# A two-layer hybrid encoder on one core: norms and gate rows spread by DMA, the feed-forward's plan started earlier and kept in order

## The chip, the core and the metric

The kernel runs on one core of one Trainium2 chip. The core has a matrix engine (TensorE, "PE" in the profile, with its weight loads as "PEld"), VectorE ("DVE"), ScalarE ("ACT"), GpSimd ("POOL") and SyncE ("SP"), each with an instruction queue of its own that it works through in order. DMAs are issued from the queues of SyncE, ScalarE and GpSimd. The metric is the device time of one execution in microseconds; lower is better.

## What is computed

Everything is float32. The stream has 512 positions of width 1024; there are two layers. Cut to its frame:

```python
for layer in range(2):
    xn = rms_norm(x, mix_norm[layer])
    if layer == 0:      # 8 heads of forgetting attention and 4 of differential attention
        mixed = fox_diff_mixer(xn, ...)
    else:               # 4 mLSTM heads, chunkwise
        mixed = mlstm_mixer(xn, ...)
    x = x + mixed
    x = x + memory_cross_attention(rms_norm(x, xattn_norm[layer]), rms_norm(mem, mem_norm[layer]), ...)
    x = x + conv_ffn(rms_norm(x, ffn_norm[layer]), ...)      # causal 3-tap conv, gelu(g) * u
return rms_norm(x, final_norm)

def rms_norm(x, gain):
    return x * rsqrt(mean(x * x, axis=-1) + 1e-6) * gain
```

The differential heads (each of width 128) and the mLSTM heads (each of width 256) have a norm of the same kind over their own width. The forgetting heads need a running sum of log-forget gates along the sequence, one row of 512 numbers per head; the mLSTM needs for each head a running maximum and a stabilizer, again one row of 512 per head.

## The kernel before

Activations lie transposed: features on the 128 partitions, the 512 positions along the free axis, so x is eight tiles `x[k]` of 128x512. A float32 product is made from three fast ones: every operand is split into a high part and a low remainder (ScalarE casts the high part, VectorE subtracts it: `split`, `sub`, L278 to L283), and `mm3` (L285 to L291) multiplies high by high, low by high and high by low. So each weight tile of 128x1024 costs a load on SyncE's queue (`raw`), a cast on ScalarE (`wh`) and a subtraction on VectorE (`wl`); each of these three has three buffers. Products are gathered in four PSUM banks `acc` and in two pairs of banks with the tags `s` and `w`.

**Order.** The program is unrolled in full. In all stages but the feed-forward, `Plan` (L80) orders work by hand: each item has a duration on TensorE and a chain of durations on ScalarE ("A"), VectorE ("D") and GpSimd ("G"), and takes and frees slots of buffers; `Plan.run` walks along TensorE's time, takes the first ready item by priority and calls its function, which issues the instructions. The feed-forward uses `Sched` (L159): tasks per engine with durations, latencies and slots, in which the engine that can start earliest is served, and ties go by priority. Both fix the order in which instructions are issued. The compiler's own scheduler then places them in the queues by that order and by its own estimate of when an operand is ready, so that a queue's order may differ from the plan's.

**Norm by columns** (`p_norm` L369, `rsqrt_cols`, `rsqrt`, `bcast_cols` L435). The squares of all feature tiles are summed into one tile `sq` on ScalarE and VectorE. Four narrow products per 512 positions sum over the partitions and leave the sums as columns (128x4). `rsqrt` computes the inverse root on VectorE with a first guess by bits and three Newton steps: twelve instructions on 128x4. `bcast_cols` splits the result, multiplies it into two diagonal 128x512 tiles on VectorE, and two wide products with a matrix of ones spread it over all partitions; a copy to SBUF by ScalarE makes `rb` where the result is kept. `self.r`, the columns, serves where positions lie on partitions (values); `self.rb` serves as a factor when products are evacuated (in `query` L1055, in `evac` L1320).

**Rows of gates.** `split_rows` (L594) splits rows into high and low parts in one tile; `bcast_row` (L607) makes a selecting matrix on VectorE and spreads one row with one wide product, and ScalarE copies it out of PSUM: once for each forgetting head (into `ta`), twice for each mLSTM head (`mxb`, and `emt` with an exponential). GpSimd cuts these tiles causally (`affine_select`, L900 and L1576) before they are used in the scores.

**Memory.** `p_memory` (L944) norms the same 256 memory positions in both layers, with each layer's gain; its `memrb` multiplies the keys.

**Feed-forward** (`ffn_steps`). 22 pairs of column blocks (g and u). Pairs 0 to 4 are plain: two blocks of 24 wide products each. From pair 5 on (`seven`) a pair is computed with seven products of a 2x2 scheme, which need sums of weight tiles: a tile `sa` is loaded on SyncE's queue and a second load from GpSimd's queue is added onto it in flight (L1340), and VectorE forms `sb` from it (L1362). The activations for this scheme are formed once (`forms`: tiles `th`, `tl`, by way of the buffers `hs` and `sa`), after pairs 0 and 1. `hs` has two buffers, shared by `forms` and by the pairs' evacuated rows; `sa` has three. After a pair, `tail` convolves (ScalarE, four VectorE taps), applies the gelu and splits. In `seven` ScalarE copies the first product out as `v` (L1394), and the next products wait for it. `fill` puts blocks of the down projection between. The norm of the feed-forward is issued after the first block of pair 0.

## Time and profile before

| | us |
|---|---|
| time, median of three runs (lowest, highest) | 1456.62 (1454.38, 1457.17) |
| profiled execution, its own time | 1456.26 |
| its span, first to last instruction | 1454.5 |
| TensorE busy | 1423.8 (98%) |
| VectorE busy | 1177.4 (81%) |
| ScalarE busy | 826.3 (57%) |
| GpSimd busy | 58.7 (4%) |

The rows shown further down are of that one profiled execution. A row of the timeline has the start and the duration in us, the engine, the line, the operation, the tiles written and read, the shapes, a count, and in brackets the idle time before it with what ended it. A row of the groups has, after the bar, busy time in us and the mean of one instruction in ns. An engine with a q behind its name (SPq) is its queue issuing a DMA. A row of DMA issues ends with KB each and the median us from issue to landing. A row of waits has the waiting instruction, what it waited for, the total in us, how often, and the longest.

### The profile page before, as it was taken

The numbers are of one execution on the slowest core, as the hardware profiler recorded it, in microseconds if no ns is written. First come the engines' busy times: TensorE is split into PE (matmuls) and PEld (weight loads), VectorE is DVE, ScalarE is ACT, GpSimd is POOL, SyncE is SP. The second block draws the span as 40 slices with busy tenths as digits, with TensorE's granted clock in tenths as the row PEclk, the third lists the DMA queues.
The fourth block names the chain that finished last, engine by engine and source line by source line (L and its number), as shares of the span: only waits on it lengthen the run. The fifth ranks groups of instructions, "written<-read, shape, count | busy, mean of one in ns | idle before, by whom it ended". The sixth has DMA issues, their size and how long they took to land.

```text
span 1454.5 us, 22322 instructions
## 1 busy us (share of the span) xinstructions
PE 1423.8 (98%) x8366; PEld 1269.8 (87%) x8366; DVE 1177.4 (81%) x2206; ACT 826.3 (57%) x1416; POOL 58.7 (4%) x101
## 2 busy tenths in 40 slices
PE   9999999999998999999999999999999989999998
PEld 7888868899887999999888788889988889999997
DVE  7778886766687999999778868676667889999985
ACT  7767574444464566666456734445445556666654
POOL 0000120000000000000000100000000000000000
PEclk9999999999999999999999999999999999999999
DMA  5222314323236566652232232323323656666412
GB/s 200 88 73 73 102 32 158 117 86 131 87 123 180 150 167 159 169 156 77 84 102 87 73 102 80 109 93 125 116 87 123 174 153 153 174 154 167 124 59 80
DMA packets 61213, 172.55 MB, mean 119 GB/s; under 512 B 6704, under 2 KB 6704, under 8 KB 61104
## 3 DMA queue, kind: packets, MB, share of 16 engines
q1 hardware_dynamic: 55344, 152.69, 31.9%
q0 software_dynamic: 4752, 17.30, 7.0%
q8 instruction: 66, 1.08, 0.3%
q10 hardware_dynamic: 1008, 1.12, 0.2%
q14 instruction: 43, 0.35, 0.1%
HBM read 168.99 MB, written 2.10 MB: 118 GB/s over the span
## 4 chain that ended last, share of the span: by engine, by line
PE 78%; DVE 13%; ACT 4%; issue 3%; DMA 2%; POOL 0%; SPq 0%; DVEq 0%; ACTq 0%; POOLq 0%
PE acc L289 15%; PE acc L291 14%; PE acc L290 14%; PE w L289 5%; PE w L290 5%; PE w L291 5%; DVE wl L279 3%; PE s L289 2%; PE s L290 2%; PE s L291 2%; PE acc L351 2%; PE acc L352 2%; PE acc L353 2%; DVE c L1285 2%; DMA sa<-in_up_dram 1%
## 5 line engine op out<-in xcount | busy, mean ns | idle before, releaser
L289 PE MATMUL acc<-xh,wh 128*128 128x512 f32 (+1 forms) x824 | 289.2, 351 | 0.0
L291 PE MATMUL acc<-xh,wl 128*128 128x512 f32 (+1 forms) x824 | 285.0, 346 | 0.0
L290 PE MATMUL acc<-xl,wh 128*128 128x512 f32 (+1 forms) x824 | 284.8, 346 | 0.0
L279 DVE TENSOR_TENSOR wl<-raw,wh 128x1024 fp32r<-128x1024 f32 (+2 forms) x200 | 239.3, 1196 | 38.2 <-ACT wh L282 35.7
L282 ACT CAST wh<-raw 128x1024 fp32r<-128x1024 f32 (+2 forms) x137 | 140.3, 1026 | 155.2 <-PE acc L290 95.8
L291 PEld LDWEIGHTS acc<-xh,wl 128*128 128x128 f32 x824 | 156.5, 190 | 14.8
L289 PEld LDWEIGHTS acc<-xh,wh 128*128 128x128 f32 x824 | 156.6, 190 | 14.3
L290 PEld LDWEIGHTS acc<-xl,wh 128*128 128x128 f32 x824 | 156.7, 190 | 14.2
L1285 DVE SCALAR_TENSOR_TENSOR c<-hs,vec,c 128x512 f32<-128x512 f32 x176 | 129.2, 746 | 2.7 <-ACT c L1278 2.6
L289 PE MATMUL w<-ah,wh 128*128 128x512 f32 x304 | 115.7, 381 | 0.0
L290 PE MATMUL w<-al,wh 128*128 128x512 f32 x304 | 115.5, 380 | 0.0
L291 PE MATMUL w<-ah,wl 128*128 128x512 f32 x304 | 115.3, 379 | 0.0
L1278 ACT ACTIVATE c<-hs,vec 128x512 f32<-128x512 f32 x88 | 67.5, 809 | 19.1 <-DVE hs L1422 9.3
L291 PEld LDWEIGHTS w<-ah,wl 128*128 128x128 f32 x304 | 57.6, 189 | 8.2
L289 PEld LDWEIGHTS w<-ah,wh 128*128 128x128 f32 x304 | 58.0, 191 | 6.7
L290 PEld LDWEIGHTS w<-al,wh 128*128 128x128 f32 x304 | 57.9, 190 | 6.6
L289 PE MATMUL acc<-mem,wh 128*128 128x256 f32 (+1 forms) x192 | 60.3, 314 | 0.0
L291 PE MATMUL acc<-mem,wl 128*128 128x256 f32 (+1 forms) x192 | 59.7, 311 | 0.0
L1299 ACT CAST ah<-c 128x512 fp32r<-128x512 f32 x44 | 27.2, 619 | 57.0 <-DVE c L1295 56.9
L290 PE MATMUL acc<-mem,wh 128*128 128x256 f32 (+1 forms) x192 | 59.6, 310 | 0.0
L512 DVE TENSOR_TENSOR x<-w,x 128x512 f32<-128x512 f32 x72 | 49.4, 686 | 7.9 <-PE w L291 7.7
L512 DVE TENSOR_TENSOR x<-acc,x 128x512 f32<-128x512 f32 x32 | 22.0, 690 | 40.4 <-PE acc L291 40.4
(373 smaller groups left out, 3810.3 us busy)
## 6 DMA issues: line engine op xcount, KB each, us to landing
raw<-in_up_dram SPq DMA_DIRECT2D x55, 512.0 KB, 3.2
sa<-in_up_dram SPq DMA_DIRECT2D x33, 512.0 KB, 4.2
sa<-in_up_dram POOLq DMA_DIRECT2D x33, 512.0 KB, 5.5
dr<-in_down_dram SPq DMA_DIRECT2D x64, 256.0 KB, 3.6
ra<-in_up_dram SPq DMA_DIRECT2D x33, 256.0 KB, 3.3
raw<-in_xk_dram SPq DMA_DIRECT2D x16, 512.0 KB, 3.2
raw<-in_wo_dram SPq DMA_DIRECT2D x16, 512.0 KB, 3.2
raw<-in_xq_dram SPq DMA_DIRECT2D x16, 512.0 KB, 3.3
```

What stands on the lines that cost most here:

```text
L279: self.nc.vector.tensor_tensor(out=lo, in0=v, in1=hi.bitcast(F32), op=ALU.subtract)
L282: self.nc.scalar.copy(hi, v)
L289: mm(out, wh, xh, start=first, stop=False, skip_group_check=parts)
L290: mm(out, wh, xl, start=False, stop=False, skip_group_check=parts)
L291: mm(out, wl, xh, start=False, stop=last, skip_group_check=parts)
L351: mm(ps, xh[k][:, ts], wh, start=(k == 0), stop=False)
L352: mm(ps, xh[k][:, ts], wl, start=False, stop=False)
L353: mm(ps, xl[k][:, ts], wh, start=False, stop=(k == 7))
L512: self.nc.vector.tensor_tensor(out=x, in0=restored(ps[:]), in1=x, op=ALU.add)
L1278: nc.scalar.activation(st["c_"][:, j, :], hs()[:, j, 2:514], AF.Identity, scale=self.col("cw", (layer * 3 + 2) * 44 + blk), bias=self.col( ...
L1285: nc.vector.scalar_tensor_tensor(out=c, in0=hs()[:, j, n : n + 512], scalar=w, in1=c, op0=ALU.mult, op1=ALU.add)
L1299: nc.scalar.copy(acts[p][0][:], u())
```

## The change

Eleven norms (four differential heads, three of four mLSTM heads, both cross-attentions, both feed-forwards) are computed by rows, `p_row_norm`: `sq` is split, two wide products with ones give the sums on every partition, ScalarE takes one row out with scale and epsilon, a DMA from ScalarE's queue turns it to 128x4, GpSimd raises it to the power -0.5, and two DMAs from GpSimd's queue write the result to DRAM and read it back spread over 128 partitions. The first VectorE instruction that reads it is pinned behind the one issued before it (`follow`). The norms that stay by columns (first, mixer of layer 1, last mLSTM head, memory of layer 0, final) get the power on GpSimd in place of the Newton steps. The gate rows are written to DRAM once and each is read back spread, by DMA from GpSimd's queue; the exponential of `emt` is taken on the rows. The memory's norm is kept in DRAM for layer 1. The differential heads have two `ta` buffers in place of three, the forgetting rows three `fb` of their own; `mxb` and `emt` have two each. In the feed-forward `Sched` starts each engine's clock ahead of TensorE's (`AHEAD`), models the end of the stage before, puts the norm first, and ScalarE's and VectorE's instructions are chained in the order of the plan (`planned`). Cut to its core:

```diff
...
+ROW_DMA, SPREAD_DMA = 2.7, 6.0
...
+ORDERED = ("vector", "scalar",)
...
             t += pick.dur
             u = t + (0.1 if pick.chain else 0.0)
             for e, d in pick.chain:
+                if e == "-":
+                    u += d
+                    continue
                 u = max(u, eng[e]) + d
...
+AHEAD = {"SP": 14.0, "POOL": 10.0, "ACT": 5.0, "DVE": 5.0}
...
-        self.slots = {r: [0.0] * n for r, n in res.items()}
+        self.slots = {r: [-AHEAD["SP"]] * n for r, n in res.items()}
...
-        now = {e: 0.0 for e in todo}
+        now = {e: -AHEAD.get(e, 0.0) for e in todo}
...
-                    at = 0.0 if e == "-" else now[e]
+                    at = max(t.after, -99.0 if e == "-" else now[e])
...
+class InOrder:
+    def __init__(self, tc, engine):
+        self.tc, self.engine = tc, engine
+        self.on, self.next, self.last = False, False, None
+        self.info = mybir.DependencyInfo(mybir.DependencyClass.NoSync, mybir.DependencyReason.SCHED_ONLY)
+    def __getattr__(self, name):
+        issue = getattr(self.engine, name)
+        def call(*a, **k):
+            i = issue(*a, **k)
+            if self.last is not None and (self.on or self.next):
+                self.tc.add_manual_dep(i.ins, self.last, self.info, reason="planned order")
+            self.last, self.next = i.ins.name, False
+            return i
+        return call
...
+    def follow(self):
+        self.next = True
...
+    def planned(self, on):
+        for c in self.chains:
+            c.on, c.last = on, None
...
+        a = pl.add(parts, 0, deps, prio, chain=(("A", 0.52), ("D", 0.6)))
+        a = pl.add(sums, 0.43, [a], prio, take=("s",), free=("s",), chain=(("A", 0.5),))
+        a = pl.add(turned, 0, [a], prio, chain=(("-", ROW_DMA),))
+        a = pl.add(lambda: st.update(d=self.row_root(st["z"])), 0, [a], prio, chain=(("G", 1.05), ("-", ROW_DMA)))
+        a = pl.add(spread, 0, [a], prio, chain=(("-", SPREAD_DMA),))
...
+        def last():
+            nc.vector.follow()
+            fin(st["rb"])
+        return pl.add(last, 0, [a, *fdeps], prio, chain=chain)
...
+    def row_parts(self, sq):
+        hi, lo = (self.til(self.sp, "sqt", dtype=F32R) for _ in range(2))
+        self.split(hi[:], lo[:], sq[:])
+        return hi, lo
+    def row_sums(self, parts, scale, eps):
+        ps = self.bank("b")
+        for i, part in enumerate(parts):
+            self.nc.tensor.matmul(banked(ps[:]), self.onesr[:], alternate(part[:]), start=i == 0, stop=i == 1)
+        row = self.til(self.sp, "sqt")
+        self.nc.scalar.activation(folded(row[0:1, :]), restored(ps[0:1, :]), AF.Copy, scale=float(scale), bias=float(eps))
+        return row
+    def row_turned(self, row):
+        z = self.til(self.sp, "z", (P, 4))
+        self.nc.scalar.dma_start(z[:], row[0:1, :].rearrange("o (p j) -> o p j", j=4))
+        return z
+    def row_root(self, z):
+        y = self.til(self.sp, "y", (P, 4))
+        self.nc.gpsimd.tensor_tensor(out=y[:], in0=z[:], in1=self.power[:], op=ALU.pow)
+        d = self.til(self.dp, "roots", (1, SEQ))
+        self.nc.gpsimd.dma_start(d[:].rearrange("o (p j) -> (o p) j", j=4), y[:])
+        return d
+    def row_spread(self, d, to):
+        rb = self.til(*to)
+        self.nc.gpsimd.dma_start(rb[:], d[0:1, :].to_broadcast([P, SEQ]))
+        return rb
...
-        nc.vector.tensor_scalar(out=y.bitcast(I32), in0=z.bitcast(I32), scalar1=-0.5, scalar2=1597463007.0, op0=ALU.mult, op1=ALU.add)
-        nc.vector.tensor_scalar(out=zh, in0=z, scalar1=-0.5, scalar2=None, op0=ALU.mult)
-        for _ in range(3):
-            nc.vector.tensor_tensor(out=a, in0=y, in1=y, op=ALU.mult)
-            nc.vector.tensor_tensor(out=a, in0=a, in1=zh, op=ALU.mult)
-            nc.vector.scalar_tensor_tensor(out=y, in0=a, scalar=1.5, in1=y, op0=ALU.add, op1=ALU.mult)
+        nc.gpsimd.tensor_tensor(out=y, in0=z, in1=self.power[:, :nt], op=ALU.pow)
...
+    def spread_cols(self, diags, n, pool, tag, bufs=2):
+        ps = self.bank("b")
+        for i, dg in enumerate(diags):
+            self.nc.tensor.matmul(banked(ps[:, :n]), self.onesr[:], alternate(dg), start=i == 0, stop=i == 1)
...
+        self.power = cp.tile([P, 4], F32, name="power")
+        nc.vector.memset(self.power[:], -0.5)
...
-    def bcast_row(self, rows, c):
-
-        ps = self.bank("b")
-        s = self.til(self.sp, "sel", (P, P), F32R)
-        self.nc.vector.tensor_copy(s[:], self.selc[:, c : c + 1].to_broadcast([P, P]))
-        self.nc.tensor.matmul(banked(ps[:]), s[:], alternate(rows[:]), start=True, stop=True)
-        return restored(ps[:])
-
+    def spread_row(self, rows, c, tile):
+        self.nc.gpsimd.dma_start(tile[:], rows[c : c + 1, :].to_broadcast([P, SEQ]))
...
             def decays():
-                f = self.log_sigmoid_sum(rows["z"], 8, mp, "ta", "tb", "tmp", NTA)
-                rows["f"] = self.split_rows(mp, f)
+                rows["f"] = self.log_sigmoid_sum(rows["z"], 8, mp, "ta", "tb", "tmp", NTA)
+                rows["d"] = self.til(self.dp, "decays", (8, SEQ), bufs=1)
+                nc.gpsimd.dma_start(rows["d"][:], rows["f"])
...
 
                     def spread(h=h, fb=fb):
-                        fps = self.bcast_row(rows["f"], h)
-                        fb["b"] = self.til(mp, "ta", bufs=NTA)
-                        nc.scalar.copy(folded(fb["b"][:]), fps)
-
-                    b = pl.add(spread, MM, [g, *qk], p + SOFT_PRIO, take=("s", "ta"), free=("s",), chain=(("A", 0.5),))
+                        fb["b"] = self.til(mp, "fb", bufs=3)
+                        self.spread_row(rows["d"], h, fb["b"])
+                    b = pl.add(spread, 0, [g], p, take=("fb",), chain=(("-", SPREAD_DMA),))
                     got = pl.add(lambda pt=pt: pt.update(t=self.til(mp, "pt", (P, 1536), bufs=3)), 0, qk, p + SOFT_PRIO, take=("pt",))
...
-                self.squares(k, raw, MEM, state)
+                if layer == 0:
+                    self.squares(k, raw, MEM, state)
...
+            self.memd = self.til(self.dp, "memroots", (1, MEM), bufs=1)
+            nc.gpsimd.dma_start(self.memd[:], rb[0:1, :])
+        def again():
+            self.memrb = self.til(mp, "memrb", (P, MEM), bufs=1)
+            nc.gpsimd.dma_start(self.memrb[:], self.memd[0:1, :].to_broadcast([P, MEM]))
 
         self.memdone = done
+        if layer:
+            self.memnorm = pl.add(again, 0, done[7], 1, chain=(("-", SPREAD_DMA),))
+            return
...
-            norm = self.x_norm(pl, 0, deps=self.xdone[7])
+            norm = self.x_row_norm(pl, 0, self.xdone[7])
...
+                    def query(ps, h=h, d=d, qs=qs):
                         tmp = self.til(mp, "tmp")
+                        if h == 0:
+                            nc.vector.follow()
                         nc.vector.scalar_tensor_tensor(out=folded(tmp[:]), in0=restored(ps[:]), scalar=0.0625, in1=folded(self.rb[:]), op0=ALU.mult, op1=ALU.mult)
...
+        X_LAST = 0.8
+        add("DVE", 0.6, None, (), -20.0, after=0.2)
+        add("ACT", 1.2, None, (), -20.0, after=1.0)
+        add("DVE", 1.3, None, (), -20.0, after=1.8)
...
+            def parts_():
+                n["p"] = [self.til(self.sp, "sqt", dtype=F32R) for _ in range(2)]
+                nc.scalar.copy(n["p"][0][:], prev["sq"][:])
+            def low():
+                self.sub(n["p"][1][:], prev["sq"][:], n["p"][0][:])
 
             def sums():
                 n["ps"] = self.bank("s")
-                for i in range(4):
-                    nc.tensor.matmul(n["ps"][:, 2 * i : 2 * i + 2], prev["sq"][:, i * P : (i + 1) * P], self.ones2[:], start=True, stop=True)
+                for i, part in enumerate(n["p"]):
+                    nc.tensor.matmul(banked(n["ps"][:]), self.onesr[:], alternate(part[:]), start=i == 0, stop=i == 1)
+            def row():
+                n["row"] = self.til(self.sp, "sqt")
+                nc.scalar.activation(folded(n["row"][0:1, :]), restored(n["ps"][0:1, :]), AF.Copy, scale=1.0 / DM, bias=EPS)
+                n["z"] = self.row_turned(n["row"])
 
             def root():
-                self.r = self.rsqrt(n["ps"], 4, 1.0 / DM, EPS)
+                n["d"] = self.row_root(n["z"])
 
             def spread():
-                self.rb = self.bcast_cols(self.r, SEQ, self.sp, "rb", 1)
-
-            a = pe(0.5, sums, (), [("s", st)])
-            b = add("DVE", 2.1, root, [a], a.prio, (), [("s", st)])
-            s2 = {}
-            c = pe(0.5, spread, [b], [("s", s2)], [("s", s2)])
-            return add("ACT", 0.52, None, [c], c.prio)
+                self.rb = self.row_spread(n["d"], self.rb_to())
+            a = add("ACT", 0.52, parts_, (), at, after=3.3)
+            a = add("DVE", 0.6, low, [a], at)
+            a = add("PE", 0.43, sums, [a], at, [("s", st)])
+            a = add("ACT", 0.6, row, [a], at, (), [("s", st)], ROW_DMA)
+            a = add("POOL", 1.05, root, [a], at, (), (), ROW_DMA)
+            return add("POOL", 1.0, spread, [a], at, (), (), SPREAD_DMA)
...
-            a = add("ACT", ACV, lambda: scaled(0), (), at, [("hs", st)])
+            a = add("ACT", ACV, lambda: scaled(0), (), at, [("hs", st)], after=X_LAST)
...
-                if p == 0 and j == 0:
-                    nonlocal normed
-                    normed = norm()
...
-        normed = None
+        normed = norm()
...
+        nc.planned(True)
         sc.run()
+        nc.planned(False)
...
-                gt["rows"] = self.split_rows(mp, mx, mt)
+                nc.scalar.activation(mt, mt, AF.Exp, scale=-1.0)
+                gt["rows"] = mx, mt
                 gt["u"] = zi
+                gt["d"] = [self.til(self.dp, n, (H, SEQ), bufs=1) for n in ("mx", "emt")]
+                for d, v in zip(gt["d"], gt["rows"]):
+                    nc.gpsimd.dma_start(d[:], v)
...
                 def most(h=h, st=st):
-                    mxp = self.bcast_row(gt["rows"], h)
-                    st["mx"] = self.til(mp, "mxb", bufs=1)
-                    nc.scalar.copy(folded(st["mx"][:]), mxp)
-
-                def emts(h=h, st=st):
-                    mtp = self.bcast_row(gt["rows"], 8 + h)
-                    st["emt"] = self.til(mp, "emt", bufs=1)
-                    nc.scalar.activation(folded(st["emt"][:]), mtp, AF.Exp, scale=-1.0)
-
-                b1 = pl.add(most, MM, [uc, qe], p, take=("s",), free=("s",), chain=(("A", 0.5),))
-                b2 = pl.add(emts, MM, [uc, qe], p + 1, take=("s",), free=("s",), chain=(("A", 0.5),))
+                    for i, n in enumerate(("mxb", "emt")):
+                        st[n] = self.til(mp, n, bufs=2)
+                        self.spread_row(gt["d"][i], h, st[n])
+                b1 = pl.add(most, 0, [uc, gk, *turn[-1:]], p, chain=(("-", SPREAD_DMA),))
+                turn.append(qe)
...
-                f = self.p_norm(pl, st, SEQ, (), 1.0 / 256, 0.0, scaled, ns, p + 3, fdeps=oe, chain=(("D", 1.32),))
+                if h < 3:
+                    f = self.p_row_norm(pl, st, 1.0 / 256, 0.0, (mp, "hrb", (P, SEQ), F32, 1), scaled, ns, p + 3, fdeps=oe, chain=(("D", 1.32),))
+                else:
+                    f = self.p_norm(pl, st, SEQ, (mp, "hrb", 1), 1.0 / 256, 0.0, lambda r, rb, st=st: st.update(rb=rb), ns, p + 3)
+                    f = pl.add(lambda scaled=scaled, st=st: scaled(st["rb"]), 0, [f, *oe], p + 3, chain=(("D", 1.32),))
...
```

More of the change, by code (lines that the diff above doesn't have):

```diff
@@ L376, in two @@
         def two():
[L377 to L380 removed]
+            fin(st["r"], self.spread_cols(st["d"], n, *done))
+        a = pl.add(one, 0.9 * n / 512, deps, prio, take=("s",), free=("s",), chain=(("D", 0.1), ("G", 1.05)), after=after)
+        b = pl.add(lambda: st.update(d=self.diag_cols(st["r"], n)), 0, [a], prio, chain=(("D", 0.2 + 1.2 * n / 512),))
@@ L442, in bcast_cols @@
         self.sub(rl, r, rh)
-        ps = self.bank("b")
-        for i, part in enumerate((rh, rl)):
+        out = []
+        for part in (rh, rl):
             dg = self.til(self.sp, "sqt", dtype=F32R)[:].rearrange("p (a b) -> p a b", b=P)
```

123 lines of the change are left out of this document (66 added, 57 removed).

## The prediction

> **What bounds the kernel now.** I read the page's busy table and chain first, then busy time by stretch, then TensorE's waits, then the timeline of the one long wait.
>
> ```profile
> span 1454.5 us, 22322 instructions
> PE 1423.8 (98%) x8366; PEld 1269.8 (87%) x8366; DVE 1177.4 (81%) x2206; ACT 826.3 (57%) x1416; POOL 58.7 (4%) x101
> PE 78%; DVE 13%; ACT 4%; issue 3%; DMA 2%; POOL 0%; SPq 0%; DVEq 0%; ACTq 0%; POOLq 0%
> ```
>
> TensorE is busy nearly throughout and carries 78% of the chain. So a matmul taken out anywhere shortens the run, unless another engine is already the limit at that place. Where it is, the stretches show (span, then TensorE, weight loads, VectorE, ScalarE, GpSimd, clock, DMA):
>
> ```profile
> 0.00:260.00 260.00, 252.41 (x1297) 209.66 (x1298) 208.02 (x576) 172.57 (x349) 18.62 (x39) 0.99 0.31 103
> 404.50:468.10 63.60, 56.61 (x277) 49.16 (x275) 53.39 (x92) 36.70 (x50) 3.21 (x4) 0.98 0.51 153
> 468.10:700.00 231.90, 231.65 (x1701) 221.14 (x1702) 218.94 (x327) 140.05 (x234) 10.61 (x13) 0.99 0.54 142
> 1105.60:1168.60 63.00, 56.55 (x275) 49.10 (x274) 53.31 (x92) 36.61 (x50) 3.05 (x4) 0.97 0.52 154
> ```
>
> Each feed-forward begins with a stretch in which TensorE idles: 63.60 - 56.61 = 7.0 us in layer 0 and 63.00 - 56.55 = 6.45 us in layer 1, together 13.4 us. The long stretch behind has no idle TensorE at all, but VectorE at 218.94 of 231.90, 94%. TensorE's own list of waits says that the 13.4 us are one wait in each layer:
>
> ```profile
> PE acc L289 <- ACT v L1394: 13.1, 2, 6.8
> PE s L452 <- DVE sqt L446: 2.9, 7, 1.0
> ```
>
> In layer 0 the timeline and the chain of waits (third row) show what made the copy `v` late:
>
> ```profile
> 413.67 23.20 SPq L1169 DMA_DIRECT2D raw<-in_up_dram  x5
> 436.96 1.69 SPq L1169 DMA_DIRECT2D sa<-in_up_dram  x2
> 444.22 10.22 DMA sa<-in_up_dram
> 450.81 0.69 DVE L1362 TENSOR_TENSOR sb<-sa,raw 128x512 f32<-128x512 f32 x1 [4.50 <-DMA sa<-in_up_dram]
> 454.46 0.69 DVE L1362 TENSOR_TENSOR sb<-sa,raw 128x512 f32<-128x512 f32 x1 [2.35 <-DMA sa<-in_up_dram]
> 464.96 0.69 DVE L279 TENSOR_TENSOR al<-c,ah 128x512 fp32r<-128x512 f32 x1
> 465.69 0.81 ACT L1278 ACTIVATE c<-hs,vec 128x512 f32<-128x512 f32 x1 [0.76 <-DVE al L279]
> 467.64 0.36 ACT L1394 ACTIVATE v<-acc 128x256 f32<-128x256 f32 x1
> ```
>
> SyncE's queue held the first `sa` load behind five `raw` loads until 436.96. The accumulate for pair 6 landed 10.22 us after its issue at 444.22. VectorE stood 4.50 + 2.35 = 6.85 us before two `sb` additions, with ready work queued behind them. After that `al` was late, ScalarE's convolution at 465.69 waited for it, and `v` stood behind that convolution. So 6.85 us of blocked VectorE became 7 us of idle TensorE: an order of queues, not a lack of work capacity.
>
> **The change part by part.**
>
> *Fewer matmuls.* A norm by columns sums the squares with four narrow products of two passes each, and spreads with two wide ones.
>
> ```profile
> 814.65 0.79 PE s L417 x8
> 408.50 1.05 PE L1218 MATMUL s<-ones,sq 128*128 128x2 f32 x8
> L612 PE MATMUL s<-rows,sel 128*128 128x512 f32 x16 | 6.1, 410 | 0.1
> 410.37 0.38 PE L289 MATMUL acc<-xh,wh 128*128 128x512 f32 x1
> 410.58 0.38 PE L290 MATMUL acc<-xl,wh 128*128 128x512 f32 x1
> ```
>
> A wide product takes 0.215 us from start to start (410.37 to 410.58; I use 0.216, as records are rounded). By rows there are two wide products and nothing narrow, so the spreading pair is replaced one for one and the x8 group goes: nine norms outside the feed-forward x 0.79 = 7.1, two inside x 1.05 = 2.1, together 9.2 us. Sixteen gate-row products go: 16 x 0.216 = 3.5. The second memory norm goes (half a group, 0.4, and two half-width products, 0.2): 0.6. Of the 2.9 us that TensorE waited for the diagonals I take 1.0 as saved, since the new low part of the split can be waited for in the same way; bounds 0 and 2.9.
>
> *Short VectorE chains.* Twelve to fourteen instructions of 0.16 and two diagonals of 0.69 leave per norm, and one subtraction of 0.69 comes: some 3 us less VectorE eleven times. Where TensorE bounds, this is covered and counts nothing. At the very end it does count:
>
> ```profile
> 1446.42 0.16 DVE L426 TENSOR_SCALAR z<-s 128x2 f32<-128x2 f32 x1 [0.76 <-PE s L417]
> 1448.38 0.16 DVE L432 SCALAR_TENSOR_TENSOR y<-a,y 128x2 f32<-128x2 f32 x1
> 1448.64 1.26 ACT L1693 ACTIVATE th<-acc,y 128x512 f32<-128x512 f32 x2 [1.08 <-DVE y L432]
> 191.88 0.30 POOL L900 TENSOR_SCALAR_AFFINE_SELECT tb<-ta 128x128 f32<-128x128 f32 x1 [2.17 <-ACT ta L889]
> 174.52 1.23 POOL L900 TENSOR_SCALAR_AFFINE_SELECT tb<-ta 128x512 f32<-128x512 f32 x2 [0.18 <-DVE sm L683]
> ```
>
> From 1446.58 to 1448.64 are 2.06 us. The trace has no power on GpSimd; its nearest rows are selections of 0.30 and, two in one row, 1.23. With two hand-overs of 0.1 the end changes by a gain of 0.6 to 1.6; I take 0.5, nearer a loss, because the operation is another, and keep -1 to 1.6.
>
> *The chain by rows, and who waits.* Split (ScalarE, VectorE), two products, a row out of PSUM, a DMA from ScalarE's queue, a power on GpSimd, a DMA out and a DMA back spread over 128 partitions, both from GpSimd's queue.
>
> ```profile
> 404.56 0.38 PE L289 MATMUL acc<-xh,wh 128*128 128x512 f32 x1
> 406.73 0.61 ACT L485 ACTIVATE sqt<-x 128x512 f32<-128x512 f32 x1
> 407.76 0.68 DVE L486 TENSOR_TENSOR sq<-sq,sqt 128x512 f32<-128x512 f32 x1
> 416.73 0.58 ACT L456 COPY rb<-s 128x512 f32<-128x512 f32 x1 [4.61 <-PE s L452]
> 417.42 1.29 DVE L1321 TENSOR_TENSOR hs<-acc,rb 128x512 f32<-128x512 f32 x2 [1.31 <-ACT rb L456]
> vec<-in_vec_dram ACTq DMA_DIRECT2D x1, 4.0 KB, 3.2
> x<-in_x_dram SPq DMA_DIRECT2D x16, 256.0 KB, 3.5
> sa<-in_up_dram POOLq DMA_DIRECT2D x33, 512.0 KB, 5.5
> 442.91 1.00 POOL L1340 DMA_DIRECT2D sa<-in_up_dram  x1 [70.58 <-PE acc L290]
> ```
>
> At the feed-forward's start the squares are complete at 408.44. Split 0.61 + 0.69, products 0.43, row 0.58 give 410.75. The DMAs have no equal in the trace: the first two lie between 3.2 and 5.5 each, the third between 3.5 (same bytes) and 5.5 (same queue, twice the bytes, added), 10.2 when crowded. I take 3.2, 3.2 and 4.5, with 0.8 for the power: 422.4, against 417.3 before. [...] From TensorE's start at 404.56 to 422.4 are 17.9 us. Four accumulators let it run four blocks of 24 products without the row: 4 x 5.18 + 0.43 = 21.2 us. So the wait is hidden with 3.3 us to spare; with 5.5, 5.5, 10.2 and 1.23 for the power it would end at 433.2, 7.4 us too late.
>
> Elsewhere the nine others feed work that is far off (the differential and mLSTM heads go into an output projection behind all heads; cross-attention has its key, value and query products to run). But their first reader is pinned in VectorE's order, and VectorE's splits of coming weights queue behind it. If every one were 2 us late (5.5 for 3.5), VectorE would lose 18 us; its idle fifth (208.02 of 260.00) and the weights split ahead absorb most. I charge 0.33 us each, 3 us; bounds 0 and 18. On GpSimd come eleven powers, 22 DMAs for norms, 19 for gate rows and 2 for the memory, by 1.00 us each (the row above) some 43 us in an engine busy 4%. Queued behind them are the selections for scores and the small fills of the mLSTM's convolution, which VectorE waits for; a misjudged landing delays those, and that lies within the 3 us.
>
> *The feed-forward's plan.* SyncE, GpSimd, ScalarE and VectorE are now planned from before TensorE's zero, and the two compute queues keep the plan's order. What this touches is the 13.4 us. The row comes 5 us later, so pair 0's convolution, the buffers that it frees and the second formed tile come later too; against this stand 3 us less VectorE work and no unplanned `sb` addition ahead of ready work. I take two thirds of the wait as gone, 9.0 us; bounds 0 and 13.4.
>
> **The sum.** 9.2 + 3.5 + 0.6 + 1.0 + 0.5 + 9.0 - 3.0 = 20.8 us. The profiled execution took 1456.26 us, 1.8 above its span and 0.36 below the median of the runs, so 1456.3 - 20.8 = 1435.5, told as 1435. With every bound at its good end: 9.2 + 3.5 + 0.6 + 2.9 + 1.6 + 13.4 = 31.2, 1425.
>
> **Rivals.**
>
> *The wait at pair 5 only moves.* For it: `sa` can be loaded only when a formed tile lets its buffer go, and that comes later with the row. Then the two norms inside that stretch gain nothing either: 7.1 + 3.5 + 0.6 + 1.0 + 0.5 - 3.0 = 9.7, so 1446.6.
>
> *The kept order blocks VectorE in the steady stretch (slower).* There 231.90 - 218.94 = 13 us are free, over 16 Strassen pairs 0.8 us each. In a queue that may not be reordered, an instruction whose input is later than planned stops everything behind it, as the two `sb` additions did. With 33 such pairs and w us of such waits in each, the price is 33 x (w - 0.8). It turns the 9.7 us into a loss from w = 1.1; at w = 1.7 it is 29.7, so 1476. Against it: the plan's 0.65 us per three products equals the trace's 3 x 0.216, and so far 231.65 of 231.90 was busy.
>
> *The row is late at both feed-forwards (slower).* At 433.2, TensorE stops 7.4 us for a bank and 0.7 for the evacuation, twice 8.1; the 13.4 stay: 1456.3 - 9.7 + 16.2 = 1462.8. It decides from a row 21.2 us after TensorE's start. For it: the 10.22 us of one accumulate while weights are loaded. [...]
>
> *It does nothing.* The order kept may equal the order that was there already, and the norms' gain may be eaten by their waits at 1 us each: 1455.
>
> **Chances.** Forecast 0.52, the wait moves 0.20, blocked order 0.14, late row 0.08, nothing 0.06. About 0.2%, 2.9 us, can be told from no change. The first two are faster, with 0.02 of the last; 0.04 of the last and 0.01 of the late row stay within it: faster 0.74, same 0.05, slower 0.21. From 1424 to 1460 leaves out some 0.15 above and 0.04 below; the forecast's own range is 1425 to 1443.
>
> **What would show it.** Right: no x8 group but in the column norms left; no wait of TensorE for `v` above 1 us; `rb` of the feed-forward landing before 21 us from TensorE's start there; 94% VectorE in the steady stretch with TensorE as busy as now. Wrong: TensorE waiting in every Strassen pair, or VectorE waits for the spread rows adding up to more than 18 us.

## The result, and the profile after

The changed kernel takes 1444.52 us (median of 4 runs, 1443.6 to 1445.15), beside 1455.84 us of the kernel before: ratio 0.9922, 95% interval 0.9905 to 0.9939. So it is faster by 11.3 us, where 20.8 were forecast. The profiled execution took 1445.15 us. From its page, the lines that answer to those of before:

```profile
span 1443.4 us, 21846 instructions
PE 1413.6 (98%) x8256; PEld 1257.5 (87%) x8256; DVE 1139.7 (79%) x1931; ACT 810.8 (56%) x1405; POOL 102.9 (7%) x159
```

TensorE has 110 matmuls less and VectorE 275 instructions less. What that bought differs from stage to stage. A stage ends here where the last block is added to the residual `x`; each number is a difference of two such starts on VectorE, in us:

| stage | before | changed | difference |
|---|---|---|---|
| mixing 0 | 263.6 | 256.5 | -7.1 |
| cross-attention 0 | 141.2 | 142.6 | +1.4 |
| feed-forward 0 | 337.6 | 332.6 | -5.0 |
| mLSTM | 222.3 | 224.4 | +2.1 |
| cross-attention 1 | 141.2 | 141.9 | +0.7 |
| feed-forward 1, to the final additions | 309.9 | 306.6 | -3.3 |
| end | 38.8 | 38.8 | 0.0 |

The feed-forwards gave 8.3 us (forecast 9.0 + 2.1 = 11.1), everything else 2.8 (forecast 20.8 - 11.1 = 9.7). The busy time by stretch of the changed kernel shows the two cross-attentions whole, and feed-forward 0 to pair 5, to pair 10 and to its end (columns as before):

```profile
256.50:399.10 142.60, 140.80 (x756) 124.78 (x755) 91.27 (x161) 66.39 (x123) 2.32 (x5) 1.00 0.33 106
955.90:1098.00 142.10, 141.01 (x757) 124.97 (x756) 91.28 (x161) 66.59 (x123) 2.31 (x5) 1.00 0.33 107
399.10:455.10 56.00, 56.00 (x278) 49.48 (x277) 46.47 (x67) 34.25 (x46) 5.48 (x6) 1.00 0.51 150
455.10:530.60 75.50, 74.21 (x531) 68.35 (x531) 73.75 (x112) 44.08 (x78) 4.26 (x5) 1.00 0.63 168
530.60:731.70 201.10, 200.31 (x1359) 186.83 (x1358) 185.47 (x276) 113.90 (x192) 7.52 (x10) 1.00 0.46 129
```

The stall at pair 5 is gone: 56.00 of 56.00 busy, at full clock. But in the five pairs behind it VectorE is at 73.75 of 75.50, 98%, and TensorE is idle for 1.3 us. TensorE is also idle in the cross-attentions, 1.8 and 1.1 us, where the kernel before was idle for 0.04 us in each of these stages of 141.2 us. The waits (us in total, times, longest) of TensorE and VectorE point to the cause:

```profile
PE s L1710 <- ACT k L262: 3.9, 2, 2.0
PE s L763 <- ACT sqt L262: 3.0, 1, 3.0
PE w L1021 <- ACT pt L262: 2.0, 1, 2.0
PE acc L340 <- ACT v L262: 0.8, 1, 0.8
DVE tmp L262 <- DMA rb<-roots: 10.3, 2, 5.5
DVE num L262 <- DMA hrb<-roots: 6.4, 3, 2.8
DVE ta L262 <- DMA hrb<-roots: 4.3, 2, 2.6
```

(Instructions issued through the new wrapper all have line 262; the tiles tell them apart.) VectorE stands 10.3 + 6.4 + 4.3 = 21.0 us before spread rows of the norms. (Of TensorE's two waits for `k` the one at 878.8 us stands behind such a reader, `num` at 875.86. The other, at the mLSTM's first scores, does not; it is taken up with the gate rows below.) Cross-attention 0 shows what one of these does, in the timeline of the changed kernel:

```profile
263.48 0.59 ACT L262 ACTIVATE sqt<-s 1x512 f32<-1x512 f32 x1 [0.50 <-PE s L471]
264.15 0.48 ACTq L262 DMA_DIRECT2D z<-sqt  x1
267.60 1.04 POOL L483 TENSOR_TENSOR y<-z,power 128x4 f32<-128x4 f32 x1 [59.50 <-DMA z<-sqt]
268.93 0.61 POOL L485 DMA_DIRECT2D roots<-y  x1 [0.29 <-POOL y L483]
272.17 0.54 POOL L490 DMA_DIRECT2D rb<-roots  x1 [2.63 <-DMA roots<-y]
277.71 0.69 DVE L262 SCALAR_TENSOR_TENSOR tmp<-acc,rb 128x512 f32<-128x512 f32 x1 [5.51 <-DMA rb<-roots]
278.32 1.22 DVE L262 TENSOR_TENSOR wl<-raw,wh 128x1024 fp32r<-128x1024 f32 x1
278.55 0.45 PE L340 MATMUL acc<-xh,wh 128*128 128x512 f32 x1 [0.92 <-DVE tmp L262]
```

From the row in PSUM (263.48) to its first use are 14.2 us. VectorE idles for 5.51 us at the reader, the low part `wl` of the next weights stands behind it, and TensorE stops for the accumulator that the reader frees.

Mixing 0 shows the dearest case. Behind a reader of `hrb` at 157.94, ScalarE's copy of the next head's row out of PSUM came at 160.87, and TensorE waited 3.0 us for that bank:

```profile
157.94 0.75 DVE L262 SCALAR_TENSOR_TENSOR ta<-ta,warm,hrb 128x512 f32<-128x512 f32 x1 [1.74 <-DMA hrb<-roots]
160.87 0.59 ACT L262 ACTIVATE sqt<-s 1x512 f32<-1x512 f32 x1
161.51 0.58 PE L763 MATMUL s<-ka,qa 128*128 128x256 f32 x1 [3.02 <-ACT sqt L262]
```

The same stretch in steps of 2 us:

```profile
158.00:160.00 2.00, 0.49 (x3) 0.08 (x1) 2.00 (x3) 1.27 (x3) 0.00 (x0) 1.00 0.36 125
160.00:162.00 2.00, 0.49 (x2) 0.49 (x3) 2.00 (x4) 1.73 (x4) 0.00 (x0) 0.87 0.21 33
162.00:164.00 2.00, 2.00 (x7) 1.64 (x7) 1.94 (x8) 1.86 (x5) 1.10 (x2) 0.50 0.60 230
164.00:166.00 2.00, 2.00 (x9) 1.68 (x8) 1.90 (x5) 1.93 (x5) 1.71 (x3) 0.77 0.00 0
166.00:168.00 2.00, 2.00 (x14) 1.72 (x13) 1.58 (x5) 1.34 (x4) 0.13 (x1) 1.00 1.01 87
```

After the pause the granted clock is 0.50: TensorE is "busy" and does half its work, wide products starting 0.43 us apart (162.09, 162.52, 162.95) where they start 0.21 to 0.22 apart behind it (165.00, 165.21, 165.43). Added up in steps of 1 us, such an episode loses 1.71 us. The changed kernel has three of them before its last 10 us, all outside the feed-forwards (at 161, 779 and 881 us), 5.1 us in all; the kernel before had one there (198 us) and two at each stall.

### The profile page after: what moved, and what is told of

It is laid out like the page before. It is cut to its first block, busy times and chain, and to the rows that moved or that the text cites. A ratio compares the mean times of both kernels' runs of the same rounds, so it can differ in the third digit from the quotient of the medians.

```text
span 1443.4 us, 21846 instructions
## 1 busy us (share of the span) xinstructions
PE 1413.6 (98%) x8256; PEld 1257.5 (87%) x8256; DVE 1139.7 (79%) x1931; ACT 810.8 (56%) x1405; POOL 102.9 (7%) x159
## 5 line engine op out<-in xcount | busy, mean ns | idle before, releaser
L262 ACT CAST wh<-raw 128x1024 fp32r<-128x1024 f32 (+2 forms) x200 | 204.3, 1023 | 208.4 <-PE acc L341 125.9
L340 PEld LDWEIGHTS acc<-xh,wh 128*128 128x128 f32 x824 | 157.5, 191 | 17.9 <-issue 2.2
L262 ACT ACTIVATE c<-hs,vec 128x512 f32<-128x512 f32 x88 | 70.9, 811 | 56.7 <-DVE hs L262 50.9
L262 DVE TENSOR_TENSOR x<-acc,x 128x512 f32<-128x512 f32 (+1 forms) x43 | 28.1, 654 | 57.0 <-PE acc L342 57.0
L342 PEld LDWEIGHTS w<-ah,wl 128*128 128x128 f32 x304 | 57.4, 189 | 10.3 <-DVE wl L262 2.4
L1466 POOL DMA_DIRECT2D sa<-in_up_dram x33 | 28.4, 862 | 425.6 <-DVE c L262 138.7
```

The lines of the kernel that those rows point to most:

```text
L262: i = issue(*a, **k)
L340: mm(out, wh, xh, start=first, stop=False, skip_group_check=parts)
L342: mm(out, wl, xh, start=False, stop=last, skip_group_check=parts)
L1466: return add("POOL", 0.0029 * cols, lambda: nc.gpsimd.dma_start(out(), src(), accum_op=ALU.add), deps, due, (), (), 6.0)
```

## The experiments

Theory A: the kept order and the early start (the plan begun ahead of TensorE, with the norm first) took the stalls away, and the missing gain is lost to norm rows that land too late for an engine that works in order. Rival B: the kept order itself gives the gain back in the steady stretch. The kernels were timed in 5 rounds each beside the kernel before, which had medians of 1455.84 to 1457.06 us; there are 4 to 11 runs of each. The sums of the stages are those of one profiled run of each kernel.

| kernel | median us | ratio to before, 95% | feed-forwards | rest |
|---|---|---|---|---|
| before | 1455.84 | 1 | 647.5 | 807.0 |
| changed | 1444.52 | 0.9905 to 0.9939 | 639.2 | 804.1 |
| e1_unkept | 1458.71 | 1.0006 to 1.0024 | 649.1 | 806.4 |
| e2_cols | 1437.44 | 0.9858 to 0.9884 | 639.0 | 797.0 |
| e3_nopins | 1448.95 | 0.9932 to 0.9964 | 639.0 | 809.0 |
| e4_gates | 1442.05 | 0.9887 to 0.9915 | 639.0 | 801.0 |
| e5_later | 1445.95 | 0.9914 to 0.9939 | 639.2 | 805.9 |
| e6_part | 1438.82 | 0.9862 to 0.9889 | 632.7 | 804.5 |
| e7_mix | 1445.39 | 0.9912 to 0.9937 | 639.7 | 802.9 |
| e8_ffcols | 1443.50 | 0.9888 to 0.9918 | 634.0 | 805.4 |
| e9_cols3 | 1428.55 | 0.9794 to 0.9821 | 631.4 | 795.5 |
| e10_cols3g | 1427.72 | 0.9789 to 0.9816 | 631.4 | 794.4 |
| e11_before_kept | 1464.67 | 1.0044 to 1.0070 | 656.3 | 806.6 |
| e12_cols3_free | 1444.47 | 0.9895 to 0.9928 | 645.3 | 796.8 |

**The order not kept.**

```
-        nc.planned(True)
+        nc.planned(False)
```

> Only the kept order of VectorE and ScalarE inside the feed-forwards is given up; the plan still begins ahead of TensorE. Theory A (the kept order is what took the two stalls at pair 5 away, and the missing part of the gain was lost outside the feed-forwards): the stalls come back at least in part, pair 5 of both feed-forwards begins 3 to 7 us later after its start, the time is 1447 to 1456 us. Rival B (the row's lead took the stalls away, and the kept order costs the 2.2 and 3.1 us that the stretch from pair 5 to the end of the feed-forward gave back): pair 5 stays where it is, the stretch behind it is 5 us shorter in sum, 1438 to 1441 us.

Measured 1458.71 us (1454.74 to 1460.66), 14 above the changed kernel: the way theory A says, but beyond its range. The busy time of feed-forward 0 to pair 5, to pair 10 and to its end:

```profile
400.60:463.00 62.40, 57.81 (x279) 50.68 (x277) 48.03 (x71) 34.72 (x47) 4.83 (x6) 0.98 0.53 151
463.00:538.80 75.80, 72.33 (x530) 68.77 (x529) 72.98 (x111) 46.05 (x77) 4.36 (x6) 0.99 0.62 165
538.80:738.30 199.50, 199.50 (x1360) 186.88 (x1359) 181.47 (x273) 116.67 (x192) 7.42 (x10) 1.00 0.46 125
```

TensorE's waits in the first two of them:

```profile
PE s L340 <- ACT wh L262: 3.8, 1, 3.8
PE acc L340 <- ACT u L262: 3.5, 1, 3.5
```

The start is 6.4 us longer than in the changed kernel, with a second pause just behind it. From pair 10 on it is 1.6 us shorter (199.5 for 201.1), which is all that rival B can claim in that layer.

**The nine norms outside the feed-forwards by columns**, with GpSimd's power kept:

```
-            norm = self.x_row_norm(pl, 0, self.xdone[7])
+            norm = self.x_norm(pl, 0, deps=self.xdone[7])
...
-                f = self.p_row_norm(pl, sq, 1.0 / P, EPS, (mp, "hrb", (P, SEQ), F32, 1), scaled, [w], p + SOFT_PRIO, chain=(("D", 0.66),))
+                f = self.p_norm(pl, sq, SEQ, (mp, "hrb", 1), 1.0 / P, EPS, lambda r, rb, hr=hr: hr.update(rb=rb), [w], p + SOFT_PRIO)
...
-                if h < 3:
+                if h < 0:
```

(The diagonals are issued together with the two products that spread them, also in the five norms that the change had left by columns; that was not run alone.)

> The nine norms outside the feed-forwards (four differential heads, three mLSTM heads, two cross-attentions) go back to columns, with GpSimd's power. Theory A (VectorE's 21 us of waits for spread rows are where the missing 9.5 us went): TensorE gets 9 x 0.79 = 7.1 us of work back, the waits of 10.3 us (rb) and most of 10.7 us (hrb) are gone with some 9 us of the path, so 1440 to 1446 us, and cross-attention 0 ends at least 1 us earlier behind the first mixing stage than in the changed kernel. Rival B (these waits lie beside TensorE's work, the loss is elsewhere): the 7.1 us come on top, 1450 to 1453 us.

Measured 1437.44 us: 7.1 us faster than the changed kernel although TensorE has the nine x8 groups back. That is theory A, and more than its range. By stage the profiled run gives 1.5 us in mixing 0, 1.9 in cross-attention 0, 2.5 in the mLSTM and 1.2 in cross-attention 1. The same two cross-attentions, by stretch:

```profile
255.10:395.70 140.60, 140.60 (x763) 125.70 (x762) 92.62 (x164) 66.46 (x122) 1.17 (x3) 1.00 0.32 106
950.20:1090.90 140.70, 140.70 (x764) 125.78 (x763) 92.68 (x165) 66.56 (x122) 1.15 (x3) 1.00 0.32 106
```

The norm's chain in the first of them, from the timeline of that kernel:

```profile
259.94 0.16 DVE L262 TENSOR_SCALAR z<-s 128x4 f32<-128x4 f32 x1 [0.47 <-PE s L538]
260.19 1.03 POOL L546 TENSOR_TENSOR y<-z,power 128x4 f32<-128x4 f32 x1 [51.22 <-DVE z L262]
265.66 0.58 ACT L262 COPY rb<-s 128x512 f32<-128x512 f32 x1 [3.49 <-PE s L573]
266.28 1.37 DVE L262 SCALAR_TENSOR_TENSOR tmp<-acc,rb 128x512 f32<-128x512 f32 x2 [2.32 <-ACT rb L262]
```

6.3 us from the sums to the reader instead of 14.2, TensorE without a gap, and no half clock anywhere before the last 3 us of the kernel. A part of this is luck: the pause of 2.1 us at the first mLSTM scores, TensorE's wait for `k`, is still there, and only missed the half clock this time (the last section says how), which is worth 1.7 us in the profiled run.

**No fixed place for the readers.**

```
     def follow(self):
-        self.next = True
+        pass
```

> The reader of a spread row is no longer tied to the place the plan gives it on VectorE; everything else is as changed, the order inside the feed-forwards too. If the tie is what costs (VectorE stands at it with the next weights' low parts behind): the 10.3 us wait on rb falls below 3 us and the time is 1438 to 1442 us. If the row itself is late for whoever needs it: the waits keep their size within a third and the time stays at 1443 to 1446 us.

Measured 1448.95 us (six runs, as far apart as 1444.62 and 1452.29), outside both ranges: 4.4 us slower than with the tie. VectorE still waits 9.5 us for `rb` and 7.4 + 7.1 for `hrb`. So the tie is not what costs; without it the readers stand no better.

**The readers placed later.**

```
+MIX_ROW, MIX_SPREAD = 4.0, 9.0
...
-        a = pl.add(turned, 0, [a], prio, chain=(("-", ROW_DMA),))
+        a = pl.add(turned, 0, [a], prio, chain=(("-", MIX_ROW),))
...
-        a = pl.add(spread, 0, [a], prio, chain=(("-", SPREAD_DMA),))
+        a = pl.add(spread, 0, [a], prio, chain=(("-", MIX_SPREAD),))
```

> Outside the feed-forwards the plan allows a row's DMA 4.0 instead of 2.7 us and the spread 9.0 instead of 6.0 us, so that the readers stand later in VectorE's order; nothing else. If the readers merely stand too early (theory A1): VectorE's wait on rb falls from 10.3 us to under 5, that on hrb from 10.7 to under 5, TensorE's two pauses of 3.2 and 2.1 us with the half clock behind them go, 1437 to 1441 us. If the row is late for the work that needs it (theory A2, the time from the squares to the landed row is too long wherever the reader stands): VectorE's waits fall, but TensorE waits for the parts instead, 1442 to 1448 us.

Measured 1445.95 us, no faster than the changed kernel. Waits of this kernel:

```profile
PE s L1711 <- ACT k L263: 7.1, 3, 3.9
DVE num L263 <- DMA hrb<-roots: 8.6, 3, 4.4
DVE tmp L263 <- DMA rb<-roots: 6.2, 2, 4.6
```

VectorE's wait on `rb` fell by 4.1 us, and cross-attention 0 by 1.7; TensorE's wait for `k` rose by 3.2, and cross-attention 1 got 3.6 us longer. For `hrb` VectorE's two waits together hardly fell (8.6 + 1.3 for 6.4 + 4.3). That agrees with theory A2: the row is late for the work, wherever its reader stands.

**The gate rows by TensorE.**

```
-                        self.spread_row(rows["d"], h, fb["b"])
+                        nc.scalar.copy(folded(fb["b"][:]), self.bcast_row(rows["f"], h))
...
-                b1 = pl.add(most, 0, [uc, gk, *turn[-1:]], p, chain=(("-", SPREAD_DMA),))
+                b1 = pl.add(most, MM, [uc, qe], p, take=("s",), free=("s",), chain=(("A", 0.5),))
```

> The 16 gate rows (forget decays, mLSTM maxima and scales) go through TensorE again instead of DMA: 16 products of 0.22 us are back, 3.5 us. Theory A for the mLSTM (TensorE's waits of 2.06 us on the mask and 2.0 us on k come of the gate rows' transfers and of their place on GpSimd's queue): mLSTM's first scores come 2 us earlier against its start, and the time is 1443 to 1446 us. Rival (those waits come of the head norms or of the conv): both waits stay, 1447 to 1449 us.

Measured 1442.05 us, 2.5 below the changed kernel and a little below theory A's range; the mLSTM took 221.8 us for 224.4, the rest as changed. The first scores came 0.8 us earlier against the stage's start (46.3 for 47.1), not 2, so the place of the gain was only partly as expected. TensorE's wait for `k` at these scores, 1.9 us in the changed kernel and 2.1 with the norms by columns, is gone here (0.2 us in all), as in the two later kernels that spread the mLSTM's gate rows by TensorE: it came with those rows.

**The order kept to 80 us of the plan only.**

```
-        sc.run()
+        sc.run(80.0, lambda: nc.planned(False))
```

> The kept order ends at 80 us of each feed-forward's plan, behind pair 5; from there the compiler's own order holds, as in the kernel whose order was not kept. If the kept order is what cost the stretch behind pair 5 its 2.2 and 3.1 us: the stretch from pair 5 to the feed-forward's last addition is 1.5 to 2.5 us shorter than in the changed kernel in each layer, pair 5 stays, 1439 to 1442 us. If that stretch is short of weights' parts whatever the order: the same as the changed kernel, 1443 to 1446 us. If the stall only moves behind the end of the kept part: a pause over 2 us near pair 6 or 7, 1447 to 1451 us.

Measured 1438.82 us. Pair 5 stays where it was and the stretch behind it is 2.8 and 3.7 us shorter, somewhat more than expected. Rival B is right to this extent: the kept order behind pair 5 costs 6.5 us in both layers (639.2 to 632.7).

**The feed-forward norms by columns**, still first and in the kept order:

```
-            a = add("ACT", 0.52, parts_, (), at, after=3.3)
...
-            return add("POOL", 1.0, spread, [a], at, (), (), SPREAD_DMA)
+            a = add("PE", 0.9, sums, (), at, [("s", st)], after=3.3)
+            a = add("DVE", 0.1, root, [a], at, (), [("s", st)])
+            a = add("POOL", 1.05, None, [a], at)
+            a = add("DVE", 1.5, diags, [a], at)
+            a = add("PE", 0.43, spread, [a], at, [("s", s2)], [("s", s2)])
+            return add("ACT", 0.52, None, [a], at)
```

> Only the two feed-forward norms go back to columns, still ahead of the first pairs and in the kept order. If the lead and the order took the stalls away and the row only saves TensorE its groups: both stalls stay gone, 2 x 1.05 us more, 1445.5 to 1447.5 us. If the 1.5 us of diagonal products on VectorE at the start of the plan bring the stall back: pair 5 over 3 us later in each layer, 1450 to 1456 us.

Measured 1443.50 us (1438.39 to 1444.67), below both expectations. The stages of the table are of a run of 1441.15 us, 2.35 below the median, so this kernel's sums flatter it. Feed-forward 0 to pair 5 and to pair 10:

```profile
399.50:455.10 55.60, 55.60 (x274) 49.11 (x274) 49.77 (x75) 34.48 (x46) 5.46 (x5) 1.00 0.55 159
455.10:528.50 73.40, 73.32 (x542) 69.47 (x541) 71.64 (x108) 43.76 (x76) 3.41 (x4) 1.00 0.62 165
```

The x8 group costs nothing up to pair 5 (55.6 for 56.0), and the next five pairs are 2.1 us shorter. VectorE's column says why: with the row it did 46.47 us of work up to pair 5 and 73.75 of 75.50 behind; with columns 49.77 and 71.64. As I read it, the row left VectorE without work early, and the work came back where it had no room.

**Columns outside and gate rows by TensorE together** (e2 with e4's edit).

> The nine norms outside the feed-forwards by columns and the 16 gate rows by TensorE together; the feed-forwards stay as changed. If the two add up (7.1 us and 2.4 us under the changed kernel, which they gave alone): 1434 to 1436.5 us. If both removed the same waits of VectorE in the mLSTM, so that the 3.5 us of gate products are no longer paid for: 1437 to 1440 us.

Measured 1445.39 us, outside both ranges: 8 us slower than the columns alone. The mLSTM gained 1.0 more (220.9 for 221.9), but mixing 0 took 262.2 us for 255.1. TensorE's longest pause there, 2.8 us at 189 us on VectorE's `x`, and the half clock behind it (1.7) make up 4.5 of these 7.1 us; why the forget heads' rows by TensorE bring that pause only beside column norms was not tried.

**All norms by columns, order kept to 80 us** (e2, e6 and e8 in one), **and the same with the mLSTM's gate rows alone by TensorE.**

> All norms by columns with GpSimd's power (nine outside, two inside the feed-forwards), the feed-forward's norm still ahead of its first pairs, order kept to 80 us of its plan. If the three parts add up as their traces have them (7.3 us for the nine, 4.0 for the two, 6.1 for the shorter kept part, of which some 2.4 are the same pauses behind pair 5 as the second's): 1444.5 less 12.6 to 17.4, 1427 to 1432 us, with no pause of TensorE over 0.9 us in the feed-forwards. If the diagonal products on VectorE need the kept order behind pair 5: a stall over 2 us returns there and 1433 to 1438 us.

> The same, and the mLSTM's eight gate rows by TensorE again; the forget heads' rows stay on DMA. If the pauses of 1.7 and 2.1 us at the mLSTM's start come of the gate rows' transfers: the mLSTM 1 to 2 us shorter than in the kernel before it in this list, 1426 to 1431 us. If the eight products of 0.22 us are the larger: 0.5 to 1.7 us longer.

Measured 1428.55 and 1427.72 us, both as added up, and both faster than either kernel of the study. The mLSTM got 0.9 us shorter by the gate products, a little less than expected. From the first one's page, and its feed-forward 0 by stretch:

```profile
span 1426.8 us, 22059 instructions
394.80:450.40 55.60, 55.60 (x275) 49.20 (x274) 49.78 (x75) 34.46 (x46) 4.78 (x5) 1.00 0.56 160
450.40:524.20 73.80, 73.61 (x543) 69.42 (x542) 72.51 (x111) 45.16 (x77) 4.46 (x6) 1.00 0.65 174
524.20:723.90 199.70, 199.48 (x1360) 187.11 (x1359) 181.65 (x273) 116.66 (x192) 7.24 (x10) 1.00 0.46 125
```

**The kernel before with the order kept**, nothing else:

```
+class InOrder:
...
+        nc.planned(True)
         sc.run()
+        nc.planned(False)
```

> The kernel before with one thing of the change: VectorE's and ScalarE's order inside the feed-forwards is kept as planned. Its plan is the old one, with the norm at pair 4 and nothing begun ahead. If the order alone removes the stalls (the compiler's own order put other work ahead of what pair 5 needs): both stalls of 7.0 and 6.45 us at most half as long, with the half clock behind them gone, 1443 to 1450 us. If it was the norm's late place and the lead: the stalls stay, 1454 to 1460 us.

Measured 1464.67 us, slower than the kernel before and outside both ranges. TensorE's waits at the start of feed-forward 0:

```profile
PE s L495 <- DVE sqt L254: 3.8, 1, 3.8
PE s L1261 <- DVE sq L254: 2.9, 1, 2.9
PE acc L332 <- ACT wh L254: 2.6, 1, 2.6
```

These three are all of TensorE's waits in this feed-forward's first 150 us, and the whole run has none for `v`. So the kept order alone does take the stall at pair 5 away. But an order that knows nothing of the work still under way (the last squares, the norm's sums) makes TensorE wait for exactly these at the start: 9.3 us in each layer for the 6.8 and 6.3 saved, and the half clock on top (0.50 for 10.2 us from 408.0 us on in layer 0, for 13.7 us from 1111.1 us on in layer 1).

**All norms by columns, order not kept at all** (e9 without it).

> The kernel with all norms by columns, with no kept order at all; the feed-forward's norm and plan still begin ahead of TensorE. If the order is what the start of the feed-forward needs, whatever form the norm has: pauses of 7 to 9 us at pair 5 of each layer, as where the changed kernel's order was given up, 1438 to 1444 us. If the norm's row was what the compiler's order went wrong on: no pauses over 2 us there, 1427 to 1431 us.

Measured 1444.47 us, with pauses of 4.9 and 5.3 us at pair 5, shorter than expected: the order is needed whatever the norm's form. The early start without the order gives 645.3 to 649.1 us in the feed-forwards, the order without the early start 656.3, neither 647.5, both 639.7 or less. The parts of the early start (the lead of the queues, the norm first, the end of the stage before in the plan) were not run apart.

## Why the prediction was half right

The direction was right. But 1444.52 us lies 1.5 above the forecast's own range (1425 to 1443) and nearer to the 1446.6 of the rival in which the wait at pair 5 only moves. That rival's mechanism is not what happened: the wait went, and the gain was lost elsewhere.

**The stall at pair 5: right.** The order took it away (it is gone in the old plan too, once that is kept), and the early start hides what the order costs at the feed-forward's beginning. TensorE's wait for `v` is 0.8 us (13.1 before). The row's spread was issued at 412.6 us and landed 4.0 later, at 416.6; TensorE's start, put as far ahead of the last addition (399.1) as before, is 398.9. That is 17.7 us, against 17.9 forecast, inside the cover of 21.2. That it came so close is partly luck: the three DMAs took 2.0, 3.0 and 4.0 us for 3.2, 3.2 and 4.5, the power 1.7 for 0.8, and the way from the squares to the row's end 3.2 for 2.3. The 9.0 itself left out terms on both sides, which partly cancel: the half clock behind the stalls (two episodes at each, 6.8 us in all) was not in the sum, and 6.5 us were given back by keeping the order too long.

**The x8 groups inside the feed-forward: wrong sign.** "Two inside x 1.05 = 2.1" became a loss: 5.2 us in the profiled runs (639.2 against 634.0 by columns), 1.0 by the medians of the runs, and 1.3 where the order was kept to 80 us only (632.7 against 631.4). All three point the same way; the size is not settled, and it overlaps the kept order's 6.5. The wait of TensorE was hidden, as argued; that VectorE's work was pushed into the next pairs is read from the stretches.

**"I charge 0.33 us each, 3 us; bounds 0 and 18": the step that failed.** Back to columns, the nine norms are 7.1 us faster while paying 9 x 0.79 = 7.1 us of TensorE again by the prediction's own price. So the rows cost some 14 us, nearly five times the charge, if that price holds, and some 7 even were the groups free. The prediction took VectorE's idle fifth as cover. It is no cover for a queue that must stand still: VectorE idled 21.0 us at these readers, above the 18 that the prediction had named as the sign of being wrong, the parts behind were late, and the half clock behind pauses, which the prediction left out, took 3.4 us more beside the norms (at 161 and 881 us; the third, at 779, belongs to the gate rows). That the reader is pinned was named as the danger; e3 and e5 speak against the pin and the reader's place. That leaves the row's lateness, 14.2 us against 6.3. No run shortened the row's chain alone, so which part of it costs (the three DMAs, the power, or ScalarE's copy of the row out of a bank that TensorE needs) stays open.

**Sixteen gate rows, 3.5 us: wrong in the changed kernel.** Given back to TensorE they make it 2.5 us faster, and the eight of the mLSTM alone 0.8 us in the kernel with all norms by columns, with runs that just overlap (1428.23 to 1428.92, and 1427.47 to 1428.29). For the eight forget rows it is open: by TensorE they cost 7 us beside column norms and nothing beside row norms.

**The diagonals' wait, 1.0: not saved.** "PE s <- DVE sqt 2.9" went, and 3.0 us on ScalarE's copy of the row out of the same bank came.

**The tail, 0.5: nothing** (38.8 in both). The second memory norm was not measured alone.

**The DMA times: near.** Issues of the changed kernel, medians to landing:

```profile
hrb<-roots POOLq DMA_DIRECT2D x7, 256.0 KB, 4.0
rb<-roots POOLq DMA_DIRECT2D x4, 256.0 KB, 4.4
z<-sqt ACTq DMA_DIRECT2D x11, 2.0 KB, 2.0
roots<-y POOLq DMA_DIRECT2D x11, 2.0 KB, 2.7
```

Forecast were 3.2 for `z`, 3.2 for `roots` and 4.5 for the spread (`hrb`, `rb`); measured 2.0, 2.7, and 4.0 to 4.4.

**The other rivals.** Kept order blocking the steady stretch was a true effect at a fraction of its price (6.5 us, not 30). A row late at both feed-forwards for TensorE, and a change that does nothing, are ruled out.

## What to carry to other kernels

Work taken off the limiting engine was no gain here where what replaced it arrived later: a norm by two small DMAs and a spread took 14.2 us where matmuls took 6.3, and its reader, before which VectorE stood idle for 5.51 us with the next weights' low part behind it, held up what TensorE needed next. Here a planned order paid only together with a plan that knew the work still under way at its start, and only over the stretch where the compiler's own order failed; behind that it cost. An engine's idle share did not tell whether it could wait: VectorE was busy for 79% of the span, and its 21.0 us of waits at these readers were not covered.

## What the hardware showed unasked

A pause of TensorE was often paid twice: behind it the granted clock fell to 0.50, and each episode cost another 1.71 us. Over all these kernels, of 18 pauses of 1.85 to 2.5 us 12 were followed by it; all but one of the longer ones were, unless the clock was already down; the pause of 1.5 us at the mLSTM's start, present in twelve kernels, never was. The pause at the first mLSTM scores (1.7 to 2.3 us) brought it in some kernels and not in others.

The traces say which. The half clock sets in at whole steps of 3.413 us, which is also how long one episode lasts (0.50 from 161.49 to 164.90 us in the changed kernel): there at 161.49, 779.31 and 881.71 us, 181 and 30 such steps apart, in the kernel before at 198.72, 464.96 and 1164.69 us, 78 and 205 apart, in e3 at 180.04 and 784.20 us, 177 apart. I divided each of the 14 traces into these steps, from 12 us behind its start to 12 us before its end. Of the steps at full clock, all 30 in which TensorE idled 1.87 us or more were followed by the half clock, and only one with less was (1.76 us, at 195 us of the kernel before); the longest idle time without it was 1.80. So in these traces it is not the pause that counts but how much of it falls into one step: 1.90 us at the first mLSTM scores of the changed kernel lay in one, the 2.11 us of the kernel with columns were divided into 1.79 and the rest. (Idle times are the profile's, in which the ends of matmuls are modelled.)
